# GpSimd adds or subtracts parts of the first up product's weight tiles, into a buffer that nothing reads

## The chip, the cores and the metric

The kernel runs on one core of one Trainium2 chip. A core has five engines with queues of their own: TensorE (PE in the profile; PEld are its weight loads), VectorE (DVE), ScalarE (ACT), GpSimd (Pool) and SyncE (SP), which here only issues transfers. Each engine works its queue in the order in which the program was built, and waits on semaphores of the others. The metric is the time of one execution on the device, in microseconds. Both kernels are launched in the same way on the same inputs.

## What is computed

A trunk of two layers on 512 tokens of width 1024, all in float32. Each layer has a mixer and a gated feed-forward part. The part that matters here is the feed-forward of the first layer:

```python
def conv_ffn(h, norm_g, w_up, conv_w, w_down):
    xn = rms_norm(h, norm_g)
    u = causal_dwconv(xn @ w_up, conv_w)
    g, val = u[..., :D_FF], u[..., D_FF:]
    return (jax.nn.silu(g) * val) @ w_down

def reference(x, ...):
    h = x
    for layer in range(2):
        if layer == 0:
            h = h + attention_mixer(h, ...)
        else:
            h = h + short_conv_mixer(h, ...)
        h = h + conv_ffn(h, ffn_norm[layer], ffn_w_up[layer], ffn_conv[layer], ffn_w_down[layer])
    return h
```

`D_FF` is 2816, so `w_up` is 1024 x 5632. "The first up product" is `xn @ w_up` of layer 0.

## The kernel before

The matrices stay close to float32 accuracy by a split: a float32 value is written as a high part (rounded to the format that TensorE reads) plus the rest. A product is then three matmuls: high by high, low by high and high by low (lines 352, 353 and 354, `mm3`).

After the attention part, which is put in order by a planner and ends at about 263 us, everything else is written as a plain loop over weight tiles. The list `wanted` holds all tiles in order of use; tile i is `wanted[i]`. Tiles 0 to 43 belong to the first up product. Tile 2j holds the 128 columns of `w_up` for block j of the gate, tile 2j + 1 those for block j of the values; each is 128 partitions x 1024 columns (eight blocks of the 1024 rows, 128 columns each). The steps of a tile are:

- SP issues its load from HBM into a `raw` buffer (line 313). There are three `raw` buffers, so the load of tile i waits until the split of tile i - 3 has been made.
- ScalarE writes the high part `whi` (line 319). There are three `whi` buffers as well, so this waits until TensorE is done with tile i - 3.
- VectorE writes the rest, `wlo` (line 320).
- TensorE runs 24 matmuls with it (`project`), into a bank of PSUM: `psa` for a gate tile, `psb` for a value tile.

`weights()` runs two tiles ahead (`AHEAD` = 2). After both tiles of a block j, `gate` turns the two banks into 128 columns of the activated product. Per bank: VectorE multiplies it by the row of norm factors (`y`, line 1178), ScalarE writes the last tap of the convolution (line 441) and VectorE adds the two others (line 444, two operations). Then ScalarE applies silu (1189), VectorE multiplies the halves (1190), and the product is split for the next matmul by ScalarE (`a_hi`, 436) and VectorE (`a_lo`, 437; the profile calls both `a`). One turn of the loop over j so holds two weight splits and one gate on VectorE, ten operations. There are 22 turns.

GpSimd has small work in the attention part only: masks, sets of single columns, and 12 copies of 128 x 512 (line 818, `y<-qr`). It has none after that.

The pool `mlp0`, which holds the activated product of layer 0 (`a_hi`, `a_lo`), is opened around the first up product and the down product behind it.

Of the kernel before, what the change touches and what calls it, by code (L numbers as in the profile page):

```python
# [17 lines left out]
F32 = mybir.dt.float32  # L18
# [4 lines left out]
ALU = mybir.AluOpType  # L23
AX = mybir.AxisListType

P = 128
S = 512
# [159 lines left out]
def trunk(  # L187
# [7 lines left out]
    act, dve, pe, pool = nc.scalar, nc.vector, nc.tensor, nc.gpsimd  # L195
# [6 lines left out]
    n_ps, pools = [0], {}  # L202

    def bank(tag):
        n_ps[0] += 1
        ps = pools["ps"]
        return ps.tile([P, S], F32, tag=tag, name=f"ps{tag}{n_ps[0]}", bufs={"a": 2, "b": 4, "c": 2}[tag])

    def f32(ap):
        return ap.bitcast(F32)  # L210
# [91 lines left out]
    def load(i):  # L302

        dram, k0, nk, parts = wanted[i]
        n = sum(parts[1::2])
        raw = wp.tile([P, CHUNK], F32, tag="raw", name=f"raw{i}")
        hi = wp.tile([P, CHUNK], F32R, tag="whi", name=f"whi{i}", bufs=3)
        lo = wp.tile([P, CHUNK], F32R, tag="wlo", name=f"wlo{i}", bufs=3)
        v = raw[:, 0:nk * n].rearrange("p (k c) -> p k c", c=n)
        to = 0  # L310
        for c0, width in zip(parts[::2], parts[1::2]):
            with nc.allow_non_contiguous_dma(reason="eight columns"):
                nc.sync.dma_start(
                    v[:, :, to:to + width], dram[k0 * P:(k0 + nk) * P, c0:c0 + width].rearrange("(k p) c -> p k c", p=P))
            to += width

        def part(a, b):
            at_ = slice(a * n, b * n)
            made = act.activation(hi[:, at_], raw[:, at_], AF.Copy)  # L319
            dve.tensor_tensor(lo[:, at_], raw[:, at_], f32(hi[:, at_]), op=ALU.subtract)  # L320
            return made
        halve[i] = part, nk
        return [t[:, 0:nk * n].rearrange("p (k c) -> p k c", c=n) for t in (hi, lo)]

    def split_all(i, last=None):
        part, nk = halve.pop(i)
        made = part(0, nk)
        if last is not None:
            behind(made, last)

    def weights(ahead=AHEAD):
        while len(ready) < min(len(wanted), at[0] + 1 + ahead):
            ready.append(load(len(ready)))
            split_all(len(ready) - 1)
        at[0] += 1
        return ready[at[0] - 1]
# [12 lines left out]
    def mm3(acc, w, rhs, first, last):  # L349

        hi, lo = (turns(x) for x in rhs)
        pe.matmul(acc, w[0], hi, start=first, stop=False)  # L352
        pe.matmul(acc, w[0], lo, start=False, stop=False)  # L353
        pe.matmul(acc, w[1], hi, start=False, stop=last)  # L354
        spend(0.65)
# [816 lines left out]
    def residual_into(o, acc, nxt):  # L1172
        own = halves_of(h[:, o, :])
        dve.tensor_tensor(own, sorted_(acc), own, op=ALU.add)
        nxt.feed(o, h[:, o, :])
# [4 lines left out]
    def up(layer, norm, a_hi, a_lo):  # L1180
        def gate(j, accs):
            u = []
            for half, acc in enumerate(accs):
                y = work.tile([P, S], F32, tag="y", name=f"y{layer}{j}{half}")
                scaled(y, acc, norm)
                t = work.tile([P, S], F32, tag=f"u{half}", name=f"u{layer}{j}{half}", bufs=2 + half)
                causal_conv(t, y, lambda i: ffn_tap(layer, i, half * NF + j))
                u.append(t)
            act.activation(u[0], u[0], AF.Silu)  # L1189
            dve.tensor_tensor(u[0], u[0], u[1], op=ALU.mult)  # L1190
            split(a_hi[:, j, :], a_lo[:, j, :], u[0])

        for j in range(NF):
            accs = []
            for half in range(2):
                accs.append(bank("ab"[half]))
                project(accs[-1], weights())
            norm.scaled(lambda j=j, accs=accs: gate(j, accs))

    def mlp_tiles(pool_):  # L1200
        return [pool_.tile([P, NF, S], F32R, tag=f"a{i}", name=f"a_{i}") for i in range(2)]

    with tc.tile_pool(name="mlp0", bufs=1) as mp:
        a_hi, a_lo = mlp_tiles(mp)
        up(0, norm, a_hi, a_lo)
        norm = Norm("n2", 16)
        for o in range(ND):
            acc = bank("ab"[o % 2])
            k = 0
            for nk in (8, 7, 7):  # L1210
                w = weights()
                for kk in range(nk):
                    mm3(acc, (w[0][:, kk, :], w[1][:, kk, :]), (a_hi[:, k, :], a_lo[:, k, :]), k == 0, k == NF - 1)
                    k += 1
            residual_into(o, acc, norm)
        norm.finish()
# [118 lines left out]
```

## The time and the profile before

| what | value |
| --- | --- |
| time, median of 2 runs | 1123.22 us (1123.0 to 1123.45) |
| the profiled execution | 1123.36 us, of which the span 1121.6 us |
| PE busy | 1110.7 us (99%) |
| DVE busy | 716.8 us (64%) |
| ACT busy | 478.4 us (43%) |
| Pool busy | 25.4 us (2%), all in the first 322 us |
| granted TensorE clock | 1.00 throughout |
| the first up product | about 264 to 491 us, a turn of the loop 10.36 us |

The span runs from the first to the last instruction of the trace; the time of the execution also has what lies before and behind. Times inside the trace count from the start of the span. A row of the timeline has its start, its length, engine, line, operation, output and inputs; in brackets stands how long the engine sat idle before it, and who ended the wait. An engine's operations overlap a little, so what an operation costs its engine is read from start to start.

### The profile page before, as it was taken

How to read it: one execution, taken by the hardware profiler on the slowest of the kernel's cores; microseconds unless marked ns; L12 is line 12 of the kernel's file. 1: busy time of each engine (PE TensorE's matmuls, PEld its weight loads, DVE VectorE, ACT ScalarE, POOL GpSimd, SP SyncE). 2: the span in 40 equal slices, each digit the busy share in tenths (PEclk: the TensorE clock that was granted, in tenths of full speed). 3: DMA queues.
4: the chain of work that ended last, by engine and by line, in shares of the span. 5: the costliest groups of instructions: out<-in, count | busy, mean ns of one | idle time of the engine just before them, and what ended most of it. 6: DMA issues, size and time to landing. Idle time of an engine off the chain costs nothing.

```text
span 1121.6 us, 14658 instructions
## 1 busy us (share of the span) xinstructions
PE 1110.7 (99%) x5757; PEld 957.7 (85%) x5757; DVE 716.8 (64%) x1117; ACT 478.4 (43%) x722; POOL 25.4 (2%) x89
## 2 busy tenths in 40 slices
PE   9999999999999999999999999999999999999998
PEld 7878878788888888888888888888888888888887
DVE  5898665757777777763334655566877777772322
ACT  6666565644544444442222332233444444442120
POOL 4000000000000000000000000000000000000000
PEclk9999999999999999999999999999999999999999
DMA  7424221122333333333333333333544333333441
GB/s 199 108 65 108 76 57 57 60 89 84 107 96 111 95 108 99 100 98 104 103 98 105 101 100 97 111 94 106 139 122 118 99 99 108 94 131 114 138 144 38
DMA packets 220933, 114.40 MB, mean 102 GB/s; under 512 B 39900, under 2 KB 213260, under 8 KB 220864
## 3 DMA queue, kind: packets, MB, share of 16 engines
q1 hardware_dynamic: 202416, 109.10, 33.6%
q10 hardware_dynamic: 18064, 4.20, 1.7%
q8 instruction: 45, 0.74, 0.3%
q0 software_dynamic: 384, 0.17, 0.1%
q14 instruction: 24, 0.20, 0.1%
HBM read 109.25 MB, written 4.19 MB: 101 GB/s over the span
## 4 chain that ended last, share of the span: by engine, by line
PE 91%; DVE 4%; ACT 3%; issue 1%; DMA 1%; SPq 0%; DVEq 0%; ACTq 0%
PE psb L352 12%; PE psb L354 11%; PE psb L353 11%; PE psa L352 10%; PE psa L354 10%; PE psa L353 10%; PE acc L352 3%; PE acc L354 3%; PE acc L353 3%; PE psa L513 2%; PE psa L514 2%; PE psa L512 2%; PE psb L513 2%; PE psb L512 2%; PE psb L514 2%; PE score L1038 1%
## 5 line engine op out<-in xcount | busy, mean ns | idle before, releaser
L319 ACT ACTIVATE whi<-raw 128x1024 fp32r<-128x1024 f32 (+1 forms) x163 | 171.0, 1049 | 279.7 <-PE psb L353 97.2
L320 DVE TENSOR_TENSOR wlo<-raw,whi 128x1024 fp32r<-128x1024 f32 (+1 forms) x163 | 196.9, 1208 | 123.7 <-ACT whi L319 123.0
L352 PE MATMUL psb<-hs_hi,whi 128*128 128x512 f32 x480 | 182.7, 381 | 0.0
L353 PE MATMUL psb<-hs_lo,whi 128*128 128x512 f32 x480 | 181.9, 379 | 0.0
L354 PE MATMUL psb<-hs_hi,wlo 128*128 128x512 f32 x480 | 181.9, 379 | 0.0
L352 PE MATMUL psa<-hs_hi,whi 128*128 128x512 f32 x416 | 158.2, 380 | 1.1 <-DVE h L1067 1.1
L353 PE MATMUL psa<-hs_lo,whi 128*128 128x512 f32 x416 | 157.7, 379 | 0.0
L354 PE MATMUL psa<-hs_hi,wlo 128*128 128x512 f32 x416 | 157.7, 379 | 0.0
L444 DVE SCALAR_TENSOR_TENSOR u<-y,taps,u 128x510 f32<-128x510 f32 (+1 forms) x176 | 130.9, 746 | 5.2 <-ACT u L441 2.4
L354 PEld LDWEIGHTS psb<-hs_hi,wlo 128*128 128x128 f32 x480 | 90.7, 189 | 12.8
L352 PEld LDWEIGHTS psb<-hs_hi,whi 128*128 128x128 f32 x480 | 90.7, 189 | 12.7
L353 PEld LDWEIGHTS psb<-hs_lo,whi 128*128 128x128 f32 x480 | 90.8, 189 | 12.7
L352 PEld LDWEIGHTS psa<-hs_hi,whi 128*128 128x128 f32 x416 | 78.6, 189 | 12.5 <-ACT whi L630 1.5
L354 PEld LDWEIGHTS psa<-hs_hi,wlo 128*128 128x128 f32 x416 | 78.6, 189 | 11.1
L353 PEld LDWEIGHTS psa<-hs_lo,whi 128*128 128x128 f32 x416 | 78.6, 189 | 11.0
L436 ACT ACTIVATE a<-u 128x512 fp32r<-128x512 f32 x44 | 27.7, 630 | 118.0 <-DVE u L1190 118.0
L441 ACT ACTIVATE u<-y,taps 128x512 f32<-128x512 f32 x88 | 62.6, 713 | 11.9 <-DVE y L1178 11.9
L1178 DVE TENSOR_TENSOR y<-psb,nrow_n 128x512 f32<-128x512 f32 x44 | 30.4, 691 | 58.1 <-PE psb L354 58.1
L1189 ACT ACTIVATE u<-u 128x512 f32<-128x512 f32 x44 | 27.7, 630 | 85.8 <-DVE u L444 85.8
L352 PE MATMUL acc<-hs_hi,whi 128*128 128x512 f32 x128 | 52.5, 410 | 0.3 <-ACT u L778 0.3
L632 DVE TENSOR_TENSOR wlo<-raw,whi 128x1024 fp32r<-128x1024 f32 (+2 forms) x41 | 43.9, 1079 | 13.7 <-ACT whi L630 13.6
L353 PE MATMUL acc<-hs_lo,whi 128*128 128x512 f32 x128 | 48.6, 380 | 0.0
(251 smaller groups left out, 1914.0 us busy)
## 6 DMA issues: line engine op xcount, KB each, us to landing
raw<-in_ffn_w_up SPq DMA_DIRECT2D x88, 512.0 KB, 3.8
raw<-in_ffn_w_down SPq DMA_DIRECT2D x30, 512.0 KB, 3.6
raw<-in_conv_w_in SPq DMA_DIRECT2D x24, 512.0 KB, 3.8
raw<-in_attn_w_in SPq DMA_DIRECT2D x20, 512.0 KB, 4.2
raw<-in_ffn_w_down SPq DMA_DIRECT2D x16, 448.0 KB, 3.4
raw<-in_attn_w_out SPq DMA_DIRECT2D x8, 512.0 KB, 3.4
raw<-in_conv_w_out SPq DMA_DIRECT2D x8, 512.0 KB, 3.6
big<-in_x SPq DMA_DIRECT2D x8, 256.0 KB, 4.8
```

What stands on the lines that cost most here:

```text
L319: made = act.activation(hi[:, at_], raw[:, at_], AF.Copy)
L320: dve.tensor_tensor(lo[:, at_], raw[:, at_], f32(hi[:, at_]), op=ALU.subtract)
L352: pe.matmul(acc, w[0], hi, start=first, stop=False)
L353: pe.matmul(acc, w[0], lo, start=False, stop=False)
L354: pe.matmul(acc, w[1], hi, start=False, stop=last)
L441: act.activation(dst, src, AF.Copy, scale=tap(2))
L444: dve.scalar_tensor_tensor(dst[:, d:], src[:, 0:S - d], tap(j), dst[:, d:], op0=ALU.mult, op1=ALU.add)
L512: pe.matmul(acc, lhs[0], w[0], start=first, stop=False)
L513: pe.matmul(acc, lhs[0], w[1], start=False, stop=False)
L514: pe.matmul(acc, lhs[1], w[0], start=False, stop=last)
L632: DVE(dve_us(per * n), lambda: dve.tensor_tensor(self.lo.tile[:, at_], self.raw.tile[:, at_], f32(self.hi.tile[:, at_]), op=ALU.subtract), ...
L1178: dve.tensor_tensor(halves_of(y), sorted_(acc), halves_of(norm.row), op=ALU.mult)
```

## The change

After the split of a weight tile a function `extra` is called. For tiles 4 to 43 it gives GpSimd one or two operations on that tile: for 4 to 15 the sum of the first and the second 512 columns of `raw`; for 16 to 27 the same sum twice; for 28 to 35 the difference of the first 512 columns of `raw` and of `whi`; for 36 to 43 the sum of the first and the second 256 columns. All write into a new buffer `unread` (two of 128 x 512 float32, in the pool `mlp0`), which nothing reads.

```diff
             made = act.activation(hi[:, at_], raw[:, at_], AF.Copy)
             dve.tensor_tensor(lo[:, at_], raw[:, at_], f32(hi[:, at_]), op=ALU.subtract)
+            extra(i, raw, hi)
             return made
...
+    def unread(n):
+        return pools["row"].tile([P, S], F32, tag="unread", name=f"unread{n}", bufs=2)
+
+    def extra(i, raw, hi):
+
+        if 4 <= i < 16:
+            pool.tensor_tensor(unread(f"a{i}"), raw[:, 0:S], raw[:, S:2 * S], op=ALU.add)
+        elif 16 <= i < 28:
+            for k in range(2):
+                pool.tensor_tensor(unread(f"b{i}{k}"), raw[:, 0:S], raw[:, S:2 * S], op=ALU.add)
+        elif 28 <= i < 36:
+            pool.tensor_tensor(unread(f"c{i}"), raw[:, 0:S], f32(hi[:, 0:S]), op=ALU.subtract)
+        elif 36 <= i < 44:
+            pool.tensor_tensor(unread(f"d{i}")[:, 0:256], raw[:, 0:256], raw[:, 256:512], op=ALU.add)
...
     with tc.tile_pool(name="mlp0", bufs=1) as mp:
+        pools["row"] = mp
         a_hi, a_lo = mlp_tiles(mp)
         up(0, norm, a_hi, a_lo)
```

The queues of TensorE, VectorE, ScalarE and SP hold the same instructions in the same order as before. GpSimd's queue ended with the last copies of the attention part (before):

```order
L818 COPY y_2825<-qr_2771 128x512 [waits DVE_49,PE_49,Pool_49]
L818 COPY y_2837<-qr_2771 128x512 [waits PE_49,Pool_49]
L1331 UNCONDITIONAL_BRANCH
```

With the change, 52 operations stand behind those copies; these are four of them, two for tiles 14 and 15 and the two for tile 16:

```order
L332 TENSOR_TENSOR unreada_3851<-raw_3845 128x512 [waits DMAHW3_49,Pool_49]
L332 TENSOR_TENSOR unreada_3884<-raw_3878 128x512 [waits DMAHW4_49,Pool_49]
L335 TENSOR_TENSOR unreadb_3933<-raw_3927 128x512 [waits DMAHW5_49,Pool_49]
L335 TENSOR_TENSOR unreadb_3935<-raw_3927 128x512 [waits Pool_49]
```

The sums wait for the tile's transfer (DMAHW) alone and for an earlier operation of GpSimd's own; the differences (tiles 28 to 35) wait for ScalarE's `whi` as well.

In SP's queue the loads of tiles 6 to 8 read like this before:

```order
L313 DMA raw_3513<-in_ffn_w_up 128x8x128 [waits DMAHW0_49,DVE_49]
L313 DMA raw_3544<-in_ffn_w_up 128x8x128 [waits DMAHW1_49,DVE_49]
L313 DMA raw_3591<-in_ffn_w_up 128x8x128 [waits DMAHW2_49,DVE_49]
```

and with the change, where tile 7 is the first to go into a buffer that GpSimd has read:

```order
L313 DMA raw_3517<-in_ffn_w_up 128x8x128 [waits DMAHW0_49,DVE_49]
L313 DMA raw_3550<-in_ffn_w_up 128x8x128 [waits DMAHW1_49,DVE_49,Pool_49]
L313 DMA raw_3599<-in_ffn_w_up 128x8x128 [waits DMAHW2_49,DVE_49,Pool_49]
```

From tile 7 to tile 46 each load so waits for GpSimd's operation on the tile three before it. On ScalarE, eight splits (tiles 31 to 38) wait for GpSimd too, since the differences read `whi`; in the mixer of the second layer, one operation each of ScalarE and TensorE waits for GpSimd's last operations, because the memory of `unread` is used again.

## The prediction

> **What bounds the kernel now.** I begin with the page: its span, the engine totals and the chain that ended last.
>
> ```profile
> span 1121.6 us, 14658 instructions
> PE 1110.7 (99%) x5757; PEld 957.7 (85%) x5757; DVE 716.8 (64%) x1117; ACT 478.4 (43%) x722; POOL 25.4 (2%) x89
> PE 91%; DVE 4%; ACT 3%; issue 1%; DMA 1%; SPq 0%; DVEq 0%; ACTq 0%
> ```
>
> TensorE holds 91% of the chain, so whatever is added counts only if a matmul waits for it. GpSimd (Pool) has 25.4 us of work, all of it before 322 us. The change adds work only in the first up product. There I take the busy times of 103.6 us, which are ten turns of its loop.
>
> ```profile
> core 0: us, PE busy (x) PEld busy (x) DVE busy (x) ACT busy (x) POOL busy (x), PEclk, DMA share, GB/s
> 358.54:462.14 103.60, 103.60 (x481) 90.72 (x481) 78.57 (x100) 47.14 (x60) 0.00 (x0) 1.00 0.35 102
> ```
>
> TensorE has no gap, Pool does nothing, VectorE (DVE) works 7.86 of every 10.36 us. One turn of VectorE, in order of time, is the table that the sum needs:
>
> ```profile
> 420.94 0.69 DVE L1178 TENSOR_TENSOR y<-psb,nrow_n 128x512 f32<-128x512 f32 x1 [1.52 <-PE psb L354]
> 421.82 1.22 DVE L320 TENSOR_TENSOR wlo<-raw,whi 128x1024 fp32r<-128x1024 f32 x1 [0.19 <-ACT whi L319]
> 422.96 1.53 DVE L444 SCALAR_TENSOR_TENSOR u<-y,taps,u 128x511 f32<-128x511 f32 x2
> 424.52 0.69 DVE L1190 TENSOR_TENSOR u<-u,u 128x512 f32<-128x512 f32 x1
> 425.92 0.69 DVE L437 TENSOR_TENSOR a<-u,a 128x512 fp32r<-128x512 f32 x1 [0.70 <-ACT a L436]
> 426.52 0.69 DVE L1178 TENSOR_TENSOR y<-psa,nrow_n 128x512 f32<-128x512 f32 x1
> 427.13 1.22 DVE L320 TENSOR_TENSOR wlo<-raw,whi 128x1024 fp32r<-128x1024 f32 x1
> 428.26 1.53 DVE L444 SCALAR_TENSOR_TENSOR u<-y,taps,u 128x511 f32<-128x511 f32 x2
> 431.30 0.69 DVE L1178 TENSOR_TENSOR y<-psb,nrow_n 128x512 f32<-128x512 f32 x1 [1.51 <-PE psb L354]
> ```
>
> From start to start: y 0.69, wait 0.19, wlo 1.14, two conv operations 1.56, product 0.70, wait 0.70, a_lo 0.60, y 0.61, wlo 1.13, two conv operations 1.53, wait 1.51; together 10.36. Two of the waits, 1.51 + 0.19 = **1.70 us a turn, are spare**: they end with TensorE or with ScalarE's split just behind it, so they shrink when VectorE falls behind. The 0.70 is a round trip to ScalarE and stays. Without the spare a turn is 8.66 us. All operations but the two y (one input in PSUM) read two buffers of SBUF.
>
> How far may VectorE fall behind before TensorE notices? The split made at 427.13 is first needed by this weight load:
>
> ```profile
> 436.49 0.19 PEld L354 LDWEIGHTS psb<-hs_hi,wlo 128*128 128x128 f32 x1
> 290.16 0.19 PEld L354 LDWEIGHTS psa<-hs_hi,wlo 128*128 128x128 f32 x1
> 283.32 1.23 DVE L320 TENSOR_TENSOR wlo<-raw,whi 128x1024 fp32r<-128x1024 f32 x1 [0.25 <-ACT whi L319]
> ```
>
> It ends at 428.35, so the **lead is 8.1 us**. At its thinnest, while the first gates are caught up, it is 290.16 - 284.55 = 5.6 us; only four added operations have come by then.
>
> **The change part by part.** It adds 52 Pool operations, and nothing is removed or reordered: 12 sums of 512 columns (weight tiles 4 to 15, two to a turn, 6 turns), 24 (tiles 16 to 27, four to a turn, 6 turns), 8 differences that also read whi (two to a turn, 4 turns) and 8 sums of 256 columns (4 turns).
>
> *The operations themselves* lie on an idle engine and cost the path nothing. Their duration matters only for what they block. The trace has such a collision between Pool and VectorE:
>
> ```profile
> L818 POOL COPY y<-qr x12: 609/616/1665, 30.1 to 209.4; 128x512 f32<-128x512 f32 x12
> 155.66 1.23 DVE L632 TENSOR_TENSOR wlo<-raw,whi 128x1024 fp32r<-128x1024 f32 x1
> 157.36 1.63 DVE L632 TENSOR_TENSOR wlo<-raw,whi 128x1024 fp32r<-128x1024 f32 x1 [0.48 <-ACT whi L630]
> 155.70 1.67 POOL L818 COPY y<-qr 128x512 f32<-128x512 f32 x1 [23.89 <-DVE qr L805]
> 155.70 2.22 POOL L818 COPY y<-qr 128x512 f32<-128x512 f32 x2 [23.89 <-DVE qr L805]
> ```
>
> A Pool copy is 0.62 us at its median. The one that starts 0.04 us into a wlo takes 1.67 us: it ends at 157.37, 0.48 us after that wlo's end (156.89). The next wlo meets the second copy and takes 1.63 instead of 1.23 us. So one waits out the other, whichever comes second, and a copy of 512 columns holds VectorE for about 0.48 us. The Trainium skill states this as a rule that speaks against the change ("SBUF — State Buffer", section "Who interferes with whom"): a VectorE instruction with two SBUF inputs and a GpSimd instruction that reads SBUF take one read interface in turn, each for its whole length. The rows above agree; if the two merely overlapped, all delays below would be zero and the time that of before.
>
> *How long does an added operation hold VectorE?* The trace has no two-input Pool operation of this size. Lower bound: the copy's 0.48 us. Upper bound: twice a whole copy, 1.23 us. I take 2 x 0.48 = **0.96 us**, one copy's hold for each input read.
>
> *Four to a turn (tiles 16 to 27).* A tile's load is issued when wlo three tiles back is done, and the sum starts when it lands:
>
> ```profile
> SPq L313 <- DVE wlo L320: 156.0, 33, 4.9
> 428.37 0.37 SPq L313 DMA_DIRECT2D raw<-in_ffn_w_up  x1
> raw<-in_ffn_w_up SPq DMA_DIRECT2D x88, 512.0 KB, 3.8
> ```
>
> So a tile lands 0.02 + 3.8 us after the end of a wlo. I lay this over the VectorE table with its spare gone, from y(psb) at 0, each operation starting where the last leaves off (a wlo ends 0.08 after that point). The turn's first wlo, 0.61 to 1.75, brings its landing to 5.65. By then the other tile's sums 3 and 4, which landed at 2.37 during the first conv operation, have each gone in front of one VectorE operation: second conv operation at 3.49 instead of 2.53, product at 5.23, **0.96 late each**. The landing at 5.65 falls in that product; sum 1 runs from 5.92 to 6.88 while ScalarE makes a_hi, and a_lo, ready at 6.63, is 0.25 late; sum 2 runs behind a_lo, from 7.48 to 8.44, under y until 8.09, and wlo is 0.35 late. That wlo ends at 9.65, its tile lands at 13.47, and the next turn began at 11.10: 2.37 again, so the picture repeats. Delay 0.96 + 0.96 + 0.25 + 0.35 = 2.52 us, turn 8.66 + 2.52 = 11.18, and VectorE falls behind 0.82 us a turn, **4.9 us in six turns**. With no overlap at all it would be 4 x 0.96 - 1.70 = 2.14 a turn, 12.8 us; with the lower hold, 4 x 0.48 = 1.92 less the overlaps, nothing.
>
> *Two to a turn (tiles 4 to 15, and 28 to 35).* At most 2 x 0.96 - 1.70 = 0.22 us a turn, 1.3 us in the first six turns; less with any overlap. The differences start with wlo itself, both released by the split on ScalarE; that costs at most the same 0.96. At a hold of 1.23 it is 0.76 a turn. *The halves (36 to 43)* cost at most 0.96 a turn, and VectorE catches up.
>
> Sum: VectorE ends some **5 to 6 us late against a lead of 8.1**, and TensorE does not wait. Cover gone, each further microsecond would be paid in full, since TensorE has no gap to give it back.
>
> *The added waits.* SP's load of a tile now also waits for Pool's sum of three tiles before; behind it in SP's queue stand only later weight loads. The sums run right after landing, long before the wlo that frees the buffer anyway. The differences can free it 0.96 us later than wlo:
>
> ```profile
> 436.26 1.06 ACT L319 ACTIVATE whi<-raw 128x1024 fp32r<-128x1024 f32 x1
> ```
>
> The tile issued at 428.37 lands by 432.2, and its split is the one half a turn (5.18 us) after the one above, at 441.4: over 9 us of room. ScalarE's waits for a difference three tiles back, and one each on ScalarE and TensorE in the second layer, for work long done, cost nothing. The first sum's many waits are for work of the attention part.
>
> Forecast: the profiled execution is 1123.36 us (span 1121.6 and 1.8 around it), 0.14 above the median 1123.22 of the timed runs. With nothing added to the path I predict **1123.4 us**.
>
> **The rivals.**
>
> *The lead is used up.* The same mechanism with longer holds or worse alignment. With no overlap and 0.96: 12.8 + 1.3 - 8.1 = 6.0 us, 1129.4. With 1.23: (4 x 1.23 - 1.70) x 6 = 19.3, the first six turns 4.6, the differences 3.0; 26.9 - 8.1 = 18.8 us, 1142. For it: VectorE's spare is only 1.70 us. Against: every overlap with the two y and the 0.70 wait (2.0 us a turn) shortens it. The Trainium skill gives a two-input sum on GpSimd some 2.6 cycles an element ("GPSIMD Engine Reference", section 3.1, side-by-side cycle accounting); at its 1.2 GHz that is an estimate of 1.11 us for 512 columns. No run so far shows it; by it the delay of a turn grows by 4 x 0.15, six turns give 8.5 us and the first part up to 3.1, and TensorE would wait 0.4 to 3.5 us: 1123.8 to 1126.9.
>
> *Slower by over 2%: Pool's holds become the clock of the stage.* 2% is 22.5 us, so VectorE must lose 22.5 + 8.1 = 30.6. With overlaps of 1.3 us a turn where four sums run and 0.6 where two do, the loss at a hold H is 6(4H - 3.0) + 10(2H - 2.3) = 44H - 41, which passes 30.6 at H = 1.63 us. At 1.9 it is 42.6 - 8.1 = 34.5 us, 1158. Against it: 1.63 is more than two and a half whole copies.
>
> *Loads come late.* If Pool's queue fell a tile behind, SP's issue would move with it. Four sums that each wait out a wlo take 4 x (0.96 + 1.14) = 8.4 of 10.36 us, so Pool keeps up; past 9 us of lateness TensorE would wait, by half a turn if one tile comes that late: 1123.4 + 5.2 = 1128.6.
>
> *Faster.* TensorE is full in these turns and no operation left its queue; nothing speaks for it.
>
> **How the numbers follow.** Forecast 0.62 (1123.4, give or take 1.5); lead used up 0.29 (1124 to 1142, most of it under 1130); late loads 0.03; slower by over 2% 0.05; faster 0.01. The range goes down to 1121.5 for the scatter between executions, and up to 1131, which takes in the no-overlap bound at 0.96 and leaves the upper half of the 1.23 case out, some 1 in 10 in all. A change of less than 2% can hardly be told from none here. Faster by over 2%: 0.01; within 2%: 0.94; slower: 0.05.
>
> **What the changed profile would show.** Right: 52 more Pool operations between about 263 and 480 us, each some 1 us or longer where it waits; wlo, conv, product or a_lo stretched by up to 1 us beside them, the y never; VectorE's 1.5 us wait for psb gone in the turns of tiles 16 to 27 and back at the end; TensorE without gaps. Wrong: weight loads of wlo that wait for VectorE late in that stretch (lead used up), raw loads released by Pool (late loads), or two-input VectorE operations of unchanged length (no collision, right time for the wrong reason).

## The result, and the profile after

The changed kernel takes 1138.26 us (1138.08 to 1138.45) against 1123.22 before: 15.0 us more, a ratio of 1.0134 with the 95% interval 1.0118 to 1.0150. The prediction (1123.4, range 1121.5 to 1131.0) was wrong. The profiled execution took 1138.08 us. Its page begins (span, engines, shares of the chain that ended last):

```profile
span 1136.3 us, 14756 instructions
PE 1114.7 (98%) x5757; PEld 956.3 (84%) x5757; DVE 751.9 (66%) x1117; ACT 474.1 (42%) x722; POOL 105.5 (9%) x141
PE 75%; DVE 15%; ACT 5%; issue 3%; DMA 1%; SPq 0%; DVEq 0%; ACTq 0%
```

TensorE's share of the chain fell from 91% to 75%, VectorE's rose from 4% to 15%: part of the program is no longer bound by TensorE. The waits of TensorE's weight loads between 300 and 500 us say who it waits for (us in total, times, longest):

```profile
PEld psb L370 <- DVE wlo L320: 15.9, 12, 2.1
PEld psb L368 <- ACT whi L319: 1.1, 4, 0.3
PEld psa L370 <- DVE wlo L320: 0.5, 2, 0.3
```

It waits for the split on VectorE; before, this stage had no such wait. SP's loads, over the same stretch, were held by GpSimd four times and for 4.5 us in all:

```profile
SPq L313 <- DVE wlo L320: 183.8, 35, 7.8
SPq L313 <- POOL unreadc L337: 4.5, 4, 1.1
```

The tiles did not come late by this: in the change no split on ScalarE waits for a load between 300 and 480 us.

The answer to the VectorE table of the prediction is one turn with four sums, in order of time:

```profile
342.92 0.69 DVE L1194 TENSOR_TENSOR y<-psb,nrow_n 128x512 f32<-128x512 f32 x1
344.71 1.23 DVE L320 TENSOR_TENSOR wlo<-raw,whi 128x1024 fp32r<-128x1024 f32 x1 [1.10 <-ACT whi L319]
345.85 3.44 DVE L460 SCALAR_TENSOR_TENSOR u<-y,taps,u 128x511 f32<-128x511 f32 x2
349.33 0.69 DVE L1206 TENSOR_TENSOR u<-u,u 128x512 f32<-128x512 f32 x1
350.72 0.99 DVE L453 TENSOR_TENSOR a<-u,a 128x512 fp32r<-128x512 f32 x1 [0.70 <-ACT a L452]
351.64 0.68 DVE L1194 TENSOR_TENSOR y<-psa,nrow_n 128x512 f32<-128x512 f32 x1
352.24 1.70 DVE L320 TENSOR_TENSOR wlo<-raw,whi 128x1024 fp32r<-128x1024 f32 x1
353.86 1.52 DVE L460 SCALAR_TENSOR_TENSOR u<-y,taps,u 128x511 f32<-128x511 f32 x2
355.30 0.68 DVE L1194 TENSOR_TENSOR y<-psb,nrow_n 128x512 f32<-128x512 f32 x1
```

The turn takes 12.38 us (342.92 to 355.30). The four sums hold VectorE for nearly as long as foreseen: the conv pair is 3.44 instead of 1.53 us, 0.96 for each of two sums; a_lo 0.99 instead of 0.69; wlo 1.70 instead of 1.22; the y keep their 0.69. Together 2.69 us, against 2.52 foreseen. One place differs: the forecast had one of the first two sums in front of the product, which here keeps its 0.69. The conv pair begins 2.93 us after the y(psb) instead of 1.75, so both sums fall into it. The wait for psb (1.51) is gone, as foreseen. **But a wait of 1.10 us in front of the first wlo has come in its place**; before, 0.19 stood there. ScalarE shows where it comes from; these are its rows at the end of this turn, and VectorE's first wlo of the next:

```profile
355.48 0.64 ACT L1205 ACTIVATE u<-u 128x512 f32<-128x512 f32 x1 [2.41 <-DVE u L460]
356.02 1.04 ACT L319 ACTIVATE whi<-raw 128x1024 fp32r<-128x1024 f32 x1
357.09 1.23 DVE L320 TENSOR_TENSOR wlo<-raw,whi 128x1024 fp32r<-128x1024 f32 x1 [1.11 <-ACT whi L319]
```

In ScalarE's queue silu (line 1205 here) stands in front of the split that this wlo needs, and silu waits for the conv pair that ends at 355.38. So behind that pair VectorE must wait for silu and split together, some 1.7 us, with only the y of 0.6 us to do. The bracket at the wlo names whi; that whi had no wait of its own left, and the instruction in front of it on ScalarE was waiting for VectorE. Before, silu was done (430.51) when that whi could start, and the whi waited for TensorE:

```profile
429.88 0.63 ACT L1189 ACTIVATE u<-u 128x512 f32<-128x512 f32 x1 [1.92 <-DVE u L444]
431.08 1.06 ACT L319 ACTIVATE whi<-raw 128x1024 fp32r<-128x1024 f32 x1 [0.57 <-PE psb L353]
```

How late VectorE ends is read from one split, that of tile 39, before and after:

```profile
458.20 1.21 DVE L320 TENSOR_TENSOR wlo<-raw,whi 128x1024 fp32r<-128x1024 f32 x1
```

```profile
480.85 1.53 DVE L320 TENSOR_TENSOR wlo<-raw,whi 128x1024 fp32r<-128x1024 f32 x1
```

It ends at 482.38 instead of 459.41, 23.0 us later; less the lead of 8.1 us, 14.9 are left, and 15.0 were lost. The other turns of the change, from y(psb) to y(psb), first with two sums, then with two differences, then with two halves:

```profile
319.09 0.68 DVE L1194 TENSOR_TENSOR y<-psb,nrow_n 128x512 f32<-128x512 f32 x1
...
330.29 0.68 DVE L1194 TENSOR_TENSOR y<-psb,nrow_n 128x512 f32<-128x512 f32 x1
...
438.69 0.69 DVE L1194 TENSOR_TENSOR y<-psb,nrow_n 128x512 f32<-128x512 f32 x1
...
450.37 0.68 DVE L1194 TENSOR_TENSOR y<-psb,nrow_n 128x512 f32<-128x512 f32 x1
...
473.28 0.68 DVE L1194 TENSOR_TENSOR y<-psb,nrow_n 128x512 f32<-128x512 f32 x1
...
483.75 0.69 DVE L1194 TENSOR_TENSOR y<-psb,nrow_n 128x512 f32<-128x512 f32 x1
```

They take 11.20, 11.68 and 10.47 us, all above TensorE's 10.36: VectorE loses ground in every turn that has added operations.

### The profile page after: what moved, and what is told of

The parts are those of the page before. It is cut to its first block, busy times and chain, and to the rows that moved or that the text cites. A ratio compares the mean times of both kernels' runs of the same rounds, so it can differ in the third digit from the quotient of the medians.

```text
span 1136.3 us, 14756 instructions
## 1 busy us (share of the span) xinstructions
PE 1114.7 (98%) x5757; PEld 956.3 (84%) x5757; DVE 751.9 (66%) x1117; ACT 474.1 (42%) x722; POOL 105.5 (9%) x141
## 4 chain that ended last, share of the span: by engine, by line
PE 75%; DVE 15%; ACT 5%; issue 3%; DMA 1%; SPq 0%; DVEq 0%; ACTq 0%
PE psb L370 9%; PE psb L368 9%; PE psb L369 9%; PE psa L368 8%; PE psa L369 8%; PE psa L370 8%; DVE u L460 5%; DVE wlo L320 4%; PE acc L368 3%; PE acc L370 2%; PE acc L369 2%; PE psa L530 2%; PE psa L528 2%; PE psa L529 2%; PE psb L528 2%
## 5 line engine op out<-in xcount | busy, mean ns | idle before, releaser
L320 DVE TENSOR_TENSOR wlo<-raw,whi 128x1024 fp32r<-128x1024 f32 (+1 forms) x163 | 206.3, 1266 | 137.1 <-ACT whi L319 136.5
L460 DVE SCALAR_TENSOR_TENSOR u<-y,taps,u 128x510 f32<-128x510 f32 (+1 forms) x176 | 154.2, 879 | 5.2 <-ACT u L457 2.4
L453 DVE TENSOR_TENSOR a<-u,a 128x512 fp32r<-128x512 f32 x44 | 32.3, 734 | 25.1 <-ACT a L452 25.1
```

The costliest lines, as they stand in the source:

```text
L453: dve.tensor_tensor(lo, src, f32(hi), op=ALU.subtract)
L460: dve.scalar_tensor_tensor(dst[:, d:], src[:, 0:S - d], tap(j), dst[:, d:], op0=ALU.mult, op1=ALU.add)
```

## The experiments

The theory after the result, called the round-trip theory below: a late turn of VectorE is not 8.66 us long but some 9.7, since it contains the way over silu and the split on ScalarE. The rivals: the holds alone fill the turn (holds theory); the added waits, SP's above all, cost the time (waits theory); the loss goes with the time held, without a lead. Where a ratio is given, it compares several executions with several of the kernel before on the same chip; the other times are of one execution each.

**e1_swap and e2_swap_alone: silu behind the split**

```diff
+    silus = {}
...
             dve.tensor_tensor(lo[:, at_], raw[:, at_], f32(hi[:, at_]), op=ALU.subtract)
+            if i // 2 - 2 in silus and i % 2 == 0:
+                behind(silus.pop(i // 2 - 2), made)
             extra(i, raw, hi)
...
-            act.activation(u[0], u[0], AF.Silu)
+            silu = act.activation(u[0], u[0], AF.Silu)
+            if layer == 0:
+                silus[j] = silu
```

e2_swap_alone is the same edit in the kernel before, without `extra`.

> The changed kernel, and on ScalarE the silu of layer 0's block j comes behind the split (whi) of tile 2j+4 instead of in front of it; VectorE's and GpSimd's queues are the same, the 52 operations too. Round-trip theory (with the change VectorE waits 1.10 us a turn for a whi that stands behind silu on ScalarE, and silu waits for VectorE's own conv operations; so a turn has 0.60 us of spare, not 1.70): the 1.10 us wait in front of the second wlo goes, a turn is about 10.2 us with two sums (hidden), 11.3 with four, 10.7 with the differences; VectorE ends 6 to 8 us late against a lead of 8.1, so 1123 to 1125 us. Holds theory (GpSimd's holds alone fill the turn, order on ScalarE does not matter): turns of 11.2, 12.4 and 11.7 us stay and the time is 1137 to 1139.

> The kernel before with the same exchange of silu and whi on ScalarE, and no GpSimd operation added. Both theories: 1123 us, within 1 us of before, since VectorE waits for TensorE in every turn anyway. If the exchange alone changed the time by more, run e1_swap would have to be read against this one.

Measured: e1_swap 1122.89 us, ratio 0.9999 (0.9989 to 1.0009); e2_swap_alone 1123.10, ratio 1.0000 (0.9991 to 1.0009). All 15 us are gone, with the same 52 operations. A turn of e1_swap with four sums, VectorE and then ScalarE:

```profile
338.99 0.69 DVE L1197 TENSOR_TENSOR y<-psb,nrow_n 128x512 f32<-128x512 f32 x1
339.59 1.22 DVE L321 TENSOR_TENSOR wlo<-raw,whi 128x1024 fp32r<-128x1024 f32 x1
340.72 2.61 DVE L463 SCALAR_TENSOR_TENSOR u<-y,taps,u 128x511 f32<-128x511 f32 x2
343.36 1.65 DVE L1211 TENSOR_TENSOR u<-u,u 128x512 f32<-128x512 f32 x1
345.71 1.00 DVE L456 TENSOR_TENSOR a<-u,a 128x512 fp32r<-128x512 f32 x1 [0.70 <-ACT a L455]
...
347.23 1.70 DVE L321 TENSOR_TENSOR wlo<-raw,whi 128x1024 fp32r<-128x1024 f32 x1
...
350.29 0.68 DVE L1197 TENSOR_TENSOR y<-psb,nrow_n 128x512 f32<-128x512 f32 x1
```

```profile
347.97 1.04 ACT L320 ACTIVATE whi<-raw 128x1024 fp32r<-128x1024 f32 x1
350.47 0.63 ACT L1208 ACTIVATE u<-u 128x512 f32<-128x512 f32 x1 [1.45 <-DVE u L463]
```

The split is done before silu starts to wait, the 1.10 us in front of wlo are gone, and the turn is 11.30 us. The holds are as long as in the change: 1.08 us in the conv pair, 0.96 at the product, 0.31 at a_lo, 0.48 at wlo. They stand where the forecast had them, one in front of the second conv operation and one in front of the product; in the change both stand in the conv pair. So VectorE is held as long as before and the loss is gone, and the holds theory falls. The prediction's 11.18 us is the turn of this kernel, not of the one it was made for.

**e3_narrow: the same waits, 8 columns**

```diff
-            pool.tensor_tensor(unread(f"a{i}"), raw[:, 0:S], raw[:, S:2 * S], op=ALU.add)
+            pool.tensor_tensor(unread(f"a{i}")[:, 0:8], raw[:, 0:8], raw[:, S:S + 8], op=ALU.add)
... the other three kinds likewise
```

> The changed kernel with all 52 GpSimd operations cut to 8 columns (the sums of 8 columns are written to the unread buffer); their number, their place and all the waits of SP, ScalarE and TensorE for them stay. Holds and round-trip theories alike: the cost comes from the length for which an operation holds VectorE, so about 0.1 us each and 1123 to 1124 us. Waits theory (the added waits, SP's loads above all, cost the time): 1136 to 1139 us as with full operations.

Measured: 1122.86 us beside 1122.94 of the kernel before. Number, place and waits of the operations cost nothing at 8 columns, and e1_swap, which has the same waits for operations of full length, loses nothing either. So the waits theory falls.

**e4_only_four and e5_without_four: the lead**

```diff
-        if 4 <= i < 16:
+        if False:
...
-        elif 28 <= i < 36:
+        elif False:
...
-        elif 36 <= i < 44:
+        elif False:
```

This is e4_only_four; e5_without_four has `elif False` at `16 <= i < 28` alone.

> Only the 24 sums of tiles 16 to 27 (four a turn, six turns); the other 28 operations are left out. Round-trip theory with a lead of 8.1 us: turns of 12.4 instead of 10.36 us, 6 x 2.03 = 12.2 us late, 12.2 - 8.1 = 4.1 us lost: 1127.5, 1126 to 1129. A loss in proportion to the time held, without a lead: these sums hold 24 x 0.97 = 23 of some 46 us, so half of the 15 us: 1130.7. The prediction's own sum (8.66 us without spare): 4.9 us late, nothing lost, 1123.4.

> The changed kernel without the 24 sums of tiles 16 to 27; the 12 sums before them, the 8 differences and the 8 halves stay. Round-trip theory with a lead of 8.1 us: the first six turns leave VectorE some 4 us late, the six free turns (9.7 us each) bring it back, the differences (11.7 us a turn) make it 5.3 late and the halves hardly more; always under 8.1, so nothing lost: 1123 us. A loss in proportion to the time held: half of 15 us, 1130.5.

Measured: e4_only_four 1128.46 us, ratio 1.0049 (1.0034 to 1.0064), 5.5 us lost; e5_without_four 1123.08, ratio 1.0000 (0.9990 to 1.0009). Each holds VectorE for about half the time of the change; a loss in proportion would be some 7.5 us in both. They lose 5.5 and nothing, not 15 together: there is a threshold, which e4_only_four passes and e5_without_four does not. In e5_without_four stand turns in which GpSimd does nothing while VectorE is still late:

```profile
349.82 0.69 DVE L1194 TENSOR_TENSOR y<-psb,nrow_n 128x512 f32<-128x512 f32 x1
351.61 1.22 DVE L320 TENSOR_TENSOR wlo<-raw,whi 128x1024 fp32r<-128x1024 f32 x1 [1.11 <-ACT whi L319]
...
359.49 0.68 DVE L1194 TENSOR_TENSOR y<-psb,nrow_n 128x512 f32<-128x512 f32 x1
```

A late turn without any hold takes 9.67 us. This is the number that the prediction had as 8.66: **the spare of a turn is 0.69 us, not 1.70**.

**e6_all_four and e7_all_four_swap: four sums everywhere**

```diff
-        if 4 <= i < 16:
+        if False:
...
-        elif 16 <= i < 28:
+        elif 4 <= i < 44:
... the other two kinds never; e7_all_four_swap has the edit of e1_swap as well
```

> Four sums a turn for all tiles 4 to 43 (80 sums of 512 columns). Round-trip theory: 20 turns of 12.4 us against 10.36, 41 us late, less the lead of 8.1: 33 us lost, 1156 (1154 to 1160). In proportion to the time held: 78 us held against 47 in the change, 15 x 78 / 47 = 25 us lost, 1148. The prediction's sum (0.82 us a turn): 16.4 - 8.1 = 8.3 us lost, 1131.

> Four sums a turn for all tiles 4 to 43, and the silu of block j behind the split of tile 2j+4 on ScalarE as in e1_swap. Round-trip theory: turns of 11.25 us, 20 x 0.9 = 18 us late, less 8.1: 10 us lost, 1133 (1131 to 1136). Holds theory, order on ScalarE does not matter: as e6_all_four.

Measured: 1157.90 and 1137.81 us beside 1123.31 of the kernel before. e6_all_four is as the round-trip theory says (34.6 us lost, 33 expected), above what a proportion to the time held gives (1148). The same 80 sums cost 20.1 us less when silu stands behind the split. A turn of e6_all_four and two of e7_all_four_swap, from y(psb) to y(psb):

```profile
324.81 0.69 DVE L1194 TENSOR_TENSOR y<-psb,nrow_n 128x512 f32<-128x512 f32 x1
...
337.28 0.68 DVE L1194 TENSOR_TENSOR y<-psb,nrow_n 128x512 f32<-128x512 f32 x1
```

```profile
401.40 0.68 DVE L1197 TENSOR_TENSOR y<-psb,nrow_n 128x512 f32<-128x512 f32 x1
...
412.70 0.69 DVE L1197 TENSOR_TENSOR y<-psb,nrow_n 128x512 f32<-128x512 f32 x1
...
423.95 0.69 DVE L1197 TENSOR_TENSOR y<-psb,nrow_n 128x512 f32<-128x512 f32 x1
```

12.47 against 11.30 and 11.25. In e7_all_four_swap the turn was as expected, but the loss of 14.5 us was not (10, at most 13): its sums begin in the turns in which the first gates are caught up, one of which takes 12.0 us there, and I had counted none of that. At its last held split VectorE is 20.8 us late against the kernel before, both counted from the start of the stage; less 8.1 that is 12.7. The other 1.8 us are nearly all TensorE's own: right behind that split its granted clock falls to 0.66 between 490 and 495 us, and up to 494.5 us its matmuls start 0.43 us apart instead of 0.22. Five microseconds at 0.66 cost some 1.7.

```profile
core 0: us, PE busy (x) PEld busy (x) DVE busy (x) ACT busy (x) POOL busy (x), PEclk, DMA share, GB/s
264.00:490.00 226.00, 216.31 (x998) 186.74 (x998) 206.57 (x208) 90.50 (x121) 133.21 (x80) 1.00 0.32 91
490.00:495.00 5.00, 4.18 (x12) 3.38 (x13) 4.93 (x7) 2.12 (x3) 0.00 (x0) 0.66 0.35 105
```

Why the clock fell is not shown. The profile of e6_all_four has such a dip too (0.91 between 460 and 480 us), and what it cost there is open; the profile of the change has none.

**e8_copies and e9_writes: what holds VectorE**

```diff
-            pool.tensor_tensor(unread(f"a{i}"), raw[:, 0:S], raw[:, S:2 * S], op=ALU.add)
+            pool.tensor_copy(unread(f"a{i}"), raw[:, 0:S])
... the other three kinds likewise
```

and in e9_writes, for all tiles 4 to 43 (twice for 16 to 27):

```diff
+                pool.tensor_tensor(t[:, 0:8], raw[:, 0:8], raw[:, S:S + 8], op=ALU.add)
+                pool.memset(t[:, 8:S], 0.0)
```

> The changed kernel with each of the 52 operations a copy that reads one input (raw, for tiles 28 to 35 whi) of the same width in place of two. One hold for each input read: 0.48 us of delay for a conv operation instead of 0.97, turns of about 10.3, 11 and 10.6 us, VectorE at most 6 us late: 1123 us. A hold that does not depend on the inputs read: as the change, 1138.

> In place of each of the 52 operations GpSimd adds 8 columns of the tile (which starts it when the tile has landed, as in the change) and then fills the other 504 columns of the unread buffer with zeros: it writes as much as the change does in tiles 4 to 35 and reads almost nothing. If VectorE is held by what GpSimd reads, its two-input operations beside a fill keep their length (conv pair 1.53 us) but for some 0.1 us, and the time is 1123 us. If a write holds it as well, each fill of some 0.5 us holds it for about 0.4 us, conv pairs of up to 2.3 us stand in the trace, and the time is still 1123 to 1124 us, since VectorE then ends at most 6 us late.

Measured: e8_copies 1122.97 us, e9_writes 1122.71, beside 1123.31 and 1123.09. Rows of VectorE with four operations a turn, first of e8_copies, then of e9_writes with GpSimd's own:

```profile
365.98 1.60 DVE L320 TENSOR_TENSOR wlo<-raw,whi 128x1024 fp32r<-128x1024 f32 x1
...
371.86 1.10 DVE L460 SCALAR_TENSOR_TENSOR u<-y,taps,u 128x511 f32<-128x511 f32 x1
```

```profile
365.47 1.53 DVE L456 SCALAR_TENSOR_TENSOR u<-y,taps,u 128x511 f32<-128x511 f32 x2
365.25 1.02 POOL L334 TENSOR_TENSOR unreade<-raw 128x8 f32<-128x8 f32 x2 [3.36 <-DMA raw<-in_ffn_w_up]
366.22 0.97 POOL L335 MEMSET unreade<- 128x504 f32 x2
```

A copy holds VectorE for 0.35 to 0.38 us (a conv operation 1.10 instead of 0.75, wlo 1.60 instead of 1.22), less than the 0.48 that I had read and clearly less than half of a sum's 0.96. Fills beside the conv pair leave it at 1.53 us: these writes hold nothing. The Trainium skill says so ("SBUF — State Buffer", section "Who interferes with whom": a two-input VectorE instruction contends with a GpSimd instruction that reads SBUF, not with one that only writes it), and these rows agree.

## Why the prediction was wrong, by its steps

- **TensorE bound, every added microsecond counts only if a matmul waits:** right. It waited for wlo in 12 weight loads of value tiles.
- **Collision of two-input operations, 0.96 us each, their places:** right but for one place (the product). 0.96 a sum in the conv pair, 0.30 at a_lo (0.25 foreseen), 0.48 at wlo (0.35 foreseen). That the size came out was luck. I had read 0.48 for one input from GpSimd's side of the collision; VectorE's own row there shows 0.40 (1.63 instead of 1.23), and e8_copies 0.35 to 0.38. Twice that is 0.70 to 0.80 us, and a sum holds VectorE for 0.96 to 1.02. The estimate of 1.11 us that the prediction works out from the cycle figure of the Trainium skill ("GPSIMD Engine Reference", section 3.1) is above what VectorE lost.
- **The spare of 1.70 us a turn: this step failed.** "Two of the waits, 1.51 + 0.19 = 1.70 us a turn, are spare: they end with TensorE or with ScalarE's split just behind it, so they shrink when VectorE falls behind." The first does; the second grew from 0.19 to 1.10 us. I took the releaser in the bracket (whi) and the one behind it in the trace of before (TensorE) for the whole cause. In ScalarE's queue stood, in front of that whi, a silu that waits for VectorE. While TensorE set the pace, the silu was done 0.57 us before that whi could start; once VectorE is late, it is the later one. e5_without_four measured the late turn at 9.67 us without any hold, and e1_swap and e7_all_four_swap showed 11.3 us with four sums when the silu is moved: what the prediction had for the turn.
- **The sum:** with 9.67 in place of 8.66 the four sums make 9.67 + 2.69 = 12.36 (12.38 measured), 2.0 us late a turn instead of 0.82; six turns 12.1 instead of 4.9.
- **Two sums a turn, "at most 0.22 us late":** wrong by the same step. Turns of 11.2 us, 0.8 us late each; the differences 11.68, 1.3 late each; the halves 10.4 to 10.5, 0.1 late each, so VectorE did not catch up there as I wrote.
- **The lead of 8.1 us and the loss in full beyond it:** right. Tile 39 gives 14.9 us against 15.0 measured; e5_without_four stays below the lead and loses nothing. The thinnest lead, 5.6 us, was misread: the load at 290.16 is one of the tile before. The split that ends at 284.55 is first needed at 291.45, so the lead there is 6.9 us. No term of the sum goes by it.

```profile
291.45 0.19 PEld L354 LDWEIGHTS psb<-hs_hi,wlo 128*128 128x128 f32 x1
```

- **The added waits:** right, free (e3_narrow, e1_swap). SP's loads did wait for four of the differences, and no split waited for a load.
- **The rivals:** the first of them, the lead used up, is what happened, and its span (1129 to 1142) held the time, though I had worked it out from longer holds and missing overlaps; the holds were not longer, and the overlaps were there. "Slower by over 2%" from a hold of 1.63 us was worked out with the wrong spare as well.

## What to carry to other kernels

Before a wait is called spare, follow its releaser one step further: read which instruction stands in front of the releaser in its own queue, and what that one waits for. If the way leads back to the engine that would be late, the wait is part of a loop between the two engines and grows when the engine falls behind. An engine that is 76% busy may so have 7% of room; moving one instruction in another engine's queue can give it back without any change in the work, as here a silu behind a split did.

## What the runs showed of the hardware

GpSimd's operations of 512 float32 columns hold a VectorE operation with two inputs in SBUF for 0.96 to 1.02 us when they read two operands (what a conv pair takes longer, shared among its sums), for 0.35 to 0.38 us when they read one, and not at all when they only write (conv pair 1.53 us beside fills). That a second input costs more than twice the hold of one I had not expected. The hold is shorter than GpSimd's own record of a sum that nothing disturbs, 1.29 us. Of the change, such a sum, and a conv pair with one sum in it (1.53 without):

```profile
275.49 1.29 POOL L332 TENSOR_TENSOR unreada<-raw 128x512 f32<-128x512 f32 x1 [5.85 <-DMA raw<-in_ffn_w_up]
310.84 2.55 DVE L460 SCALAR_TENSOR_TENSOR u<-y,taps,u 128x511 f32<-128x511 f32 x2
```
